# Where split weights and activations start inside a partition of SBUF, in a float32r transformer block

## The chip, the cores and the metric

The kernel runs on one core of a Trainium2 chip. The metric is device time in microseconds (us). The kernel before took 2280.99 us, the median of three runs (2273.52 to 2281.04).

## The reference

One residual block on x (256 tokens x 2048), all in float32, every part wrapped in RMSNorms:

```
h = rmsnorm(x);  x = x + 0.5 * rmsnorm((silu(h @ w_gate) * (h @ w_up)) @ w_down)      # FFN 1, width 5632
h = rmsnorm(x)
proj = h @ w_in                     # forgetting attention q,k,v,f; differential attention q,k,v; memory q
y_fox, y_diff, y_mem = three attentions over 256 tokens (the last over 256 memory tokens)
gates = sigmoid(h @ w_merge_gate + b)                                                  # 3 x 2048
merged = g_fox * (y_fox @ w_fox) + g_diff * (y_diff @ w_diff) + g_mem * (y_mem @ w_mem)
x = x + rmsnorm(merged @ w_out)
h = rmsnorm(x);  x = x + 0.5 * rmsnorm((silu(h @ w_gate2) * (h @ w_up2)) @ w_down2)    # FFN 2
```

The weights are over 400 MB; each is read once. The bulk of the arithmetic is matrix products of 256 tokens with these weights.

## The kernel before, in words

**Split operands.** A float32 operand is used as two float32r parts, hi (the rounded value, written by ScalarE) and lo (the rest, written by VectorE). Weights come by DMA in tiles of 128 partitions x 2048 values (`raw`, three buffers). `Stream.ahead` (lines 71 to 94) splits each half of such a tile into a `hi` and a `lo` tile of 1024 values, in four buffers each, or, for three pieces of the `out` projection, in buffers of an extra pool. Activations are kept transposed as tiles `[P, k, 2, 256]`: for each block k of 128 channels a row of 256 hi values and a row of 256 lo values, 2048 bytes in all.

**Two forms of product.** `mm_a` (lines 193 to 198) has a 128x128 block of a weight stationary and streams activations. First hi of the weight against the 512 columns hi and lo of the activation, then lo of the weight against the 256 hi columns. This pair is called a pair below. `mm_b` (lines 231 to 240) has a 128x128 block of an activation stationary and streams weights: three products of 512 columns (428 in the projection `v`): hi by hi, hi by lo, lo by hi. This is called a triple.

**Stages in order.** FFN 1 gate and up (`mm_a` on `hT1`, 1408 pairs); FFN 1 down (`mm_b` on `gh1`); memory keys and values (`mm_b` on `mha`, `mhb`); projection `v` (`mm_b` on `h2T`, width 428); queries, keys and merge gates (`mm_a` on `h2T`, 1088 pairs) with the branch products (`mm_a` on `y_a`, `y_b`, 128 pairs each) and the attentions between them; `out` (`mm_b` on `mT`); FFN 2 gate and up (`mm_a` on `h3T`, 1408 pairs); FFN 2 down (`mm_b` on `gh2`). By the loops that makes 4160 pairs, 2688 streamed products of 512 columns in `mm_b` and 576 of 428 columns.

**What sets the order.** The schedule is written by hand: each engine runs its instructions in the order of the program text. TensorE takes a weight piece once ScalarE and VectorE have split it; `Stream` loads and splits ahead as far as buffers are free.

**Where tiles lie.** The pools place tiles one behind the other in each partition; nothing asks for more than the pools' default. In the built program of the kernel before, the byte address in the partition at which a tile starts, modulo 256, is:

| tile | role in mm_a | role in mm_b | start mod 256, before |
|---|---|---|---|
| hi, lo (4 buffers each) | stationary | streamed | 224 |
| hi, lo of the extra pool (3 each) | - | streamed in `out` | 192 |
| second 428-wide row of a piece of `v` | - | streamed | 144 |
| hT1 | streamed | - | 192 |
| h2T | streamed | stationary in `v` | 128 |
| h3T | streamed | - | 128 |
| y_a / y_b | streamed | - | 192 / 128 |
| mha / mhb | - | stationary | 192 / 128 |
| gh1 / gh2 | - | stationary | 128 / 192 |
| mT | - | stationary | 128 |

Inside a tile the stationary blocks step by 512 bytes and the streamed activation rows by 2048, so that within a pair the start of the streamed row less that of the weight block, modulo 1024, alternates between two values: 480 and 992 for hT1 and y_a, 160 and 672 for h2T, h3T and y_b.

Of the kernel before, what the change touches and what calls it, by code (L numbers as in the profile page):

```python
# [8 lines left out]
F32 = mybir.dt.float32  # L9
F32R = mybir.dt.float32r  # L10
BF16 = mybir.dt.bfloat16
AF = mybir.ActivationFunctionType
ALU = mybir.AluOpType
# [3 lines left out]
P = 128  # L17
D = 2048
S = 256
KT = D // P  # L20
FF = 5632
FT = FF // P
NB = 428
EPS = 1e-6
LAM_INIT = 0.8 - 0.6 * math.exp(-0.3 * 0)
NEG = -1e30

C_G1, C_GM, C_GMEM, C_G2, C_B, C_HG = 0, 16, 32, 48, 64, 112
N_COLS = 113
# [2 lines left out]
class Stream:  # L32
# [33 lines left out]
    def ahead(self, most=8):  # L66

        for _ in range(most):
            if self.done == len(self.plan):
                break  # L70
            _, r, half, extra = self.plan[self.done]
            if extra:
                if self.extra_pool is None:
                    break
                pool, tag = self.extra_pool, "x"
            else:
                if sum(not p[3] for p in self.plan[self.used:self.done]) == self.split_bufs:
                    break
                pool, tag = self.split_pool, ""
            self.load()  # L80
            w = self.aps[r].shape[-1] // 2
            src = self.raw[r][:, half * w:(half + 1) * w]
            hi = pool.tile([P, D // 2], F32R, tag="hi" + tag, name="hi")
            lo = pool.tile([P, D // 2], F32R, tag="lo" + tag, name="lo")
            n = 2 if self.done == 0 else 1
            for i in range(n):
                o = slice(i * w // n, (i + 1) * w // n)
                self.nc.scalar.copy(out=hi[:, o], in_=src[:, o])  # L88
                self.nc.vector.tensor_tensor(out=lo[:, o], in0=src[:, o], in1=hi[:, o].bitcast(F32), op=ALU.subtract)  # L89
            self.split[self.done] = (hi, lo)  # L90
            self.left[r] -= 1
            if not self.left[r]:
                del self.raw[r]
            self.done += 1
        self.load()
# [16 lines left out]
def tile_block(ctx, tc, x, mem, f1gu, f1d, wqk, wv, wmkv, wgate, wbr, wout, f2gu, f2d,  # L112
               cols, rows, lamv, fbias, cf, cb, rope, out):
    nc = tc.nc
# [74 lines left out]

    fill = Fillers(3, 2)  # L190


    def mm_a(bank, w, kk, act, k, start, stop):

        hi, lo = w
        nc.tensor.matmul(bank, lhsT=hi[:, kk * P:(kk + 1) * P], rhs=act[:, k].rearrange("p s n -> p (s n)"),  # L196
                         start=start, stop=False)
        nc.tensor.matmul(bank[:, 0:S], lhsT=lo[:, kk * P:(kk + 1) * P], rhs=act[:, k, 0], start=False, stop=stop)  # L198

    def new_bank(name):  # L200
        return mmp.tile([P, 512], F32, tag="mm", name=name)
# [27 lines left out]
    def mm_b(bank, piece, w, act, t, k0, start, stop):  # L229

        hi, lo = piece
        for kk in range(2):
            xh = act[:, k0 + kk, 0, t * P:(t + 1) * P]
            xl = act[:, k0 + kk, 1, t * P:(t + 1) * P]
            wh = hi[:, kk * w:(kk + 1) * w]
            wl = lo[:, kk * w:(kk + 1) * w]
            o = bank[:, 0:w]
            nc.tensor.matmul(o, lhsT=xh, rhs=wh, start=start and kk == 0, stop=False)  # L238
            nc.tensor.matmul(o, lhsT=xh, rhs=wl, start=False, stop=False)  # L239
            nc.tensor.matmul(o, lhsT=xl, rhs=wh, start=False, stop=stop and kk == 1)  # L240
# [42 lines left out]
    def rstd_of(acc, n, name):  # L283
# [3 lines left out]
        nc.vector.reduce_sum(out=ms, in_=acc, axis=AX.X)  # L287
        nc.vector.tensor_scalar(out=ms, in0=ms, scalar1=1.0 / n, scalar2=EPS, op0=ALU.mult, op1=ALU.add)
        rsqrt(r, ms)
# [45 lines left out]
    class PostProj:  # L335
# [24 lines left out]
        def body(self):  # L360
# [6 lines left out]
            for t in range(2):  # L367
                ssq = small.tile([P, 1], F32, tag="ssq", name="ssq_post")
                self.base[t] = small.tile([P, 1], F32, tag="base", name="base")
                nc.vector.reduce_sum(out=ssq, in_=self.acc[t][:, 0:3], axis=AX.X)  # L370
                nc.vector.tensor_scalar(out=self.base[t], in0=ssq, scalar1=f / D, scalar2=f * EPS,
                                        op0=ALU.mult, op1=ALU.add)
# [62 lines left out]
    hpool = h1_stack.enter_context(tc.tile_pool(name="hT1", bufs=1, side="right", reuse_waits="tile"))  # L435
    tp1 = h1_stack.enter_context(tc.tile_pool(name="ft1", bufs=1, side="right", reuse_waits="tile"))
    gp1 = g1_stack.enter_context(tc.tile_pool(name="gh1", bufs=1, side="left", reuse_waits="tile"))
    hT1 = hpool.tile([P, KT, 2, S], F32R, name="hT1")
    gh1 = gp1.tile([P, FT, 2, S], F32R, name="gh1")

    def load_x(c):
        for t in range(2):
# [25 lines left out]
    yap = ya_stack.enter_context(tc.tile_pool(name="yap", bufs=1, side="right", reuse_waits="tile"))  # L468
    fg_stack = ExitStack()
    fgp = fg_stack.enter_context(tc.tile_pool(name="fg1", bufs=1, side="right", reuse_waits="tile"))  # L470
    mha = yap.tile([P, 8, 2, S], F32R, tag="y", name="mha")
    macc = [small.tile([P, 4], F32, name=f"macc{t}", bufs=1) for t in range(2)]
    order = [(c, t) for c in range(4) for t in range(2)]
    mem_c = {}
# [27 lines left out]
    h2_stack = ExitStack()  # L502
    h2p = h2_stack.enter_context(tc.tile_pool(name="h2p", bufs=1, side="left", reuse_waits="tile"))
    ybp = yb_stack.enter_context(tc.tile_pool(name="ybp", bufs=1, side="left", reuse_waits="tile"))
    h2T = h2p.tile([P, KT, 2, S], F32R, tag="h", name="h2T")
    mhb = ybp.tile([P, 8, 2, S], F32R, tag="y", name="mhb")

    def x1_update(i):
        if i < 8:
# [158 lines left out]

        return [s1, s2]

    y_a = yap.tile([P, 8, 2, S], F32R, tag="y", name="y_a")
    y_b = ybp.tile([P, 8, 2, S], F32R, tag="y", name="y_b")

    def softmax_stats(s_aps, tag="e", bufs=6):

# [60 lines left out]
    def diff_unit(h):  # L736
# [22 lines left out]
        def s3():  # L759
# [12 lines left out]
            f = (1.0 - LAM_INIT) ** -2  # L772
            nc.vector.tensor_scalar(out=ms, in0=ms, scalar1=f / P, scalar2=f * EPS, op0=ALU.mult, op1=ALU.add)
            rsqrt(r, ms)
# [40 lines left out]
    for n in range(6):  # L815
        banks = proj_b("v", h2T, KT, NB)
        if n == 0:
            hrow = row_of(hr, h2p)
        for a, b, dst in segs:
            lo_c, hi_c = max(a, n * NB), min(b, (n + 1) * NB)  # L820
            if lo_c < hi_c:
                for t in range(2):
                    o, i = dst(t, lo_c - a, hi_c - a), banks[t][:, lo_c - n * NB:hi_c - n * NB]
                    if t == 0:
# [30 lines left out]
    mT = None  # L855
    for m in range(KT):
        zs = []
        for b in range(3):
            z = zp.tile([P, S], F32, tag="z", name="z", bufs=4)
            lr_sum(z, proj_a("gate", h2T), zp)  # L860
            times_row(z, hrow)
            zs.append(z)
        if m == 0:
            while fill.left():
                fill(drain=True)
            at_stack.close()
            mgp = mg_stack.enter_context(tc.tile_pool(name="mgp", bufs=1, side="left", reuse_waits="tile"))
            mT = mgp.tile([P, KT, 2, S], F32R, name="mT")
        bb = [new_bank("mm_br") for _ in range(3)]
        lims = [(0, 8), (8, 12), (12, 16)]  # L870
        for half in range(2):
            st.ahead()
            w, = st.take("br")
            for kk in range(8):
                k = half * 8 + kk
                i = 0 if k < 8 else (1 if k < 12 else 2)
                mm_a(bb[i], w, kk, (y_a, y_b)[half], kk, k == lims[i][0], k == lims[i][1] - 1)
            st.release()
        acc = None
        for b in range(3):  # L880
            g = zs[b]
            c = C_B + b * KT + m
            nc.scalar.activation(out=g, in_=g, func=AF.Sigmoid, bias=colt[:, c:c + 1])
            br = zp.tile([P, S], F32, tag="br", name="br")
            lr_sum(br, bb[b], zp)
            nc.vector.tensor_tensor(out=g, in0=br, in1=g, op=ALU.mult)
            if acc is not None:
                nc.vector.tensor_tensor(out=g, in0=acc, in1=g, op=ALU.add)
            acc = g
        split_to(mT[:, m, 0], mT[:, m, 1], acc)  # L890
# [1 line left out]
    ya_stack.close()  # L892


    h3T = h2p.tile([P, KT, 2, S], F32R, tag="h", name="h3T")
    fg_stack = ExitStack()
    fgp = fg_stack.enter_context(tc.tile_pool(name="fgm", bufs=1, side="right", reuse_waits="tile"))
    st.extra_pool = fg_stack.enter_context(tc.tile_pool(name="xsplit", bufs=3, side="right", reuse_waits="tile"))
# [28 lines left out]
    def setup2():  # L927
        row = row_of(h3r, h2p)
        fg_stack.close()
        mg_stack.close()  # L930
        yb_stack.close()
        tp = tp2_stack.enter_context(tc.tile_pool(name="ft2", bufs=1, side="left", reuse_waits="tile"))
        gp = g2_stack.enter_context(tc.tile_pool(name="gh2", bufs=1, side="right", reuse_waits="tile"))
        return row, tp, gp.tile([P, FT, 2, S], F32R, name="gh2")

    gh2 = ffn_up(2, h3T, lambda: h3r.extend(token_rstd(x_sb, t) for t in range(2)), setup2,
                 {1: lambda: (splits.pop(0)(), post2.update(1, 2), st.ahead(1)), 2: lambda: (turn(2), post2.update(1, 3)),
                  4: lambda: (splits.pop(0)(), st.ahead(1)), 5: lambda: turn(3), 8: lambda: splits.pop(0)(),
                  10: lambda: st.ahead(2)})
# [96 lines left out]
```

## Time and profile before

| | us |
|---|---|
| median of three runs | 2280.99 |
| the profiled execution | 2281.44 |
| its span, first to last instruction | 2279.6 |
| TensorE matmul busy | 2260.3 (99%) |
| TensorE weight load busy | 1939.0 (85%) |
| VectorE busy | 1407.3 (62%) |
| ScalarE busy | 1104.3 (48%) |
| DMA engines, mean share of queue 1 | 52.3% |

A busy share says how much of the span had at least one instruction of the engine under way. A matmul's listed duration includes a tail in which the next one already streams, so that durations add up to more than the time; how far one start lies from the next is the number to read. "L196" is line 196 of the kernel; the same line of the changed kernel has a larger number.

### The profile page before, as it was taken

What the parts mean: (1) busy time and instruction counts of PE and PEld (TensorE: products, weight loads), DVE (VectorE), ACT (ScalarE), POOL (GpSimd) and SP (SyncE); (2) the same over time, 40 slices, a digit from 0 to 9 for tenths busy, and PEclk for the clock granted to TensorE, in tenths of its full rate; (3) what the DMA queues carried; (4) which work ended last, traced back from release to release, by engine and by line L of the source; (5) the groups of instructions that cost most, each with busy time, mean ns of one, the idle gap of its engine ahead of it and who ended that gap; (6) DMA issues with size and microseconds to landing.
All of it is one profiled execution on the core that took longest, in us unless ns stands there. A gap on an engine that the chain in (4) does not pass through costs nothing. (4 is left out here: it accounts for less than half of the span.)

```text
span 2279.6 us, 30353 instructions
## 1 busy us (share of the span) xinstructions
PE 2260.3 (99%) x12028; PEld 1939.0 (85%) x12028; DVE 1407.3 (62%) x1969; ACT 1104.3 (48%) x1704; POOL 11.4 (0%) x22
## 2 busy tenths in 40 slices
PE   8999999999999999999999999999999999999998
PEld 7888888888888899888888888878888888888886
DVE  6666666665444656766776767566666666654444
ACT  6444444444433554444555555446544544443342
POOL 0000000000000000000000000000000000000000
PEclk9999999999999999999999999999999999999999
DMA  6555555556555554444555555545555555555553
GB/s 224 189 187 189 189 188 186 185 185 217 192 193 198 176 175 162 165 159 155 178 185 188 182 203 178 203 155 203 185 187 194 193 185 189 197 193 192 196 196 129
DMA packets 63646, 423.15 MB, mean 186 GB/s; under 512 B 7440, under 2 KB 7824, under 8 KB 16144
## 3 DMA queue, kind: packets, MB, share of 16 engines
q1 hardware_dynamic: 59616, 415.33, 52.3%
q10 hardware_dynamic: 3888, 5.88, 0.8%
q8 instruction: 94, 1.54, 0.3%
q14 instruction: 48, 0.39, 0.1%
HBM read 419.09 MB, written 2.10 MB: 185 GB/s over the span
## 5 line engine op out<-in xcount | busy, mean ns | idle before, releaser
L89 DVE TENSOR_TENSOR lo<-raw,hi 128x1024 fp32r<-128x1024 f32 (+2 forms) x793 | 942.8, 1211 | 469.7 <-ACT hi L88 426.2
L88 ACT CAST hi<-raw 128x1024 fp32r<-128x1024 f32 (+2 forms) x793 | 814.7, 1039 | 397.8 <-PE mm_b L240 322.5
L196 PE MATMUL mm_a<-hT,hi 128*128 128x512 f32 x1408 | 499.7, 398 | 2.9 <-DVE hT L321 2.9
L196 PE MATMUL mm_a<-h3T,hi 128*128 128x512 f32 x1408 | 489.7, 392 | 1.0 <-DVE h3T L321 1.0
L198 PE MATMUL mm_a<-hT,lo 128*128 128x256 f32 x1408 | 397.5, 282 | 0.9 <-DVE lo L89 0.9
L198 PE MATMUL mm_a<-h3T,lo 128*128 128x256 f32 x1408 | 394.0, 280 | 0.0
L196 PE MATMUL mm_a<-h2T,hi 128*128 128x512 f32 x1088 | 384.1, 395 | 0.0
L196 PEld LDWEIGHTS mm_a<-hT,hi 128*128 128x128 f32 x1408 | 265.1, 188 | 68.7 <-ACT hi L88 3.5
L196 PEld LDWEIGHTS mm_a<-h3T,hi 128*128 128x128 f32 x1408 | 264.9, 188 | 59.6 <-ACT tg L313 1.2
L198 PE MATMUL mm_a<-h2T,lo 128*128 128x256 f32 x1088 | 304.2, 280 | 0.0
L238 PE MATMUL mm_b<-hi,gh 128*128 128x512 f32 x704 | 279.7, 397 | 0.0
L394 ACT ACTIVATE left<-mm_a 128x256 f32<-128x256 f32 x244 | 93.8, 384 | 382.3 <-PE mm_a L198 382.3
L240 PE MATMUL mm_b<-hi,gh 128*128 128x512 f32 x704 | 277.7, 394 | 0.0
L239 PE MATMUL mm_b<-lo,gh 128*128 128x512 f32 x704 | 277.2, 394 | 0.0
L198 PEld LDWEIGHTS mm_a<-hT,lo 128*128 128x128 f32 x1408 | 266.1, 189 | 2.2 <-DVE lo L89 2.2
L198 PEld LDWEIGHTS mm_a<-h3T,lo 128*128 128x128 f32 x1408 | 264.8, 188 | 0.1
L196 PEld LDWEIGHTS mm_a<-h2T,hi 128*128 128x128 f32 x1088 | 204.4, 188 | 43.8
L198 PEld LDWEIGHTS mm_a<-h2T,lo 128*128 128x128 f32 x1088 | 204.4, 188 | 0.2
L240 PEld LDWEIGHTS mm_b<-hi,gh 128*128 128x128 f32 x704 | 132.1, 188 | 33.4
L239 PEld LDWEIGHTS mm_b<-lo,gh 128*128 128x128 f32 x704 | 132.1, 188 | 31.5
L238 PEld LDWEIGHTS mm_b<-hi,gh 128*128 128x128 f32 x704 | 132.1, 188 | 31.3
L396 DVE TENSOR_TENSOR up<-mm_a,left 128x256 f32<-128x256 f32 x88 | 37.3, 424 | 75.9 <-ACT left L394 75.9
(205 smaller groups left out, 1781.0 us busy)
## 6 DMA issues: line engine op xcount, KB each, us to landing
raw<-in_f2gu SPq DMA_DIRECT2D x88, 1024.0 KB, 4.8
raw<-in_f1gu SPq DMA_DIRECT2D x86, 1024.0 KB, 4.8
raw<-in_wgate SPq DMA_DIRECT2D x48, 1024.0 KB, 4.7
raw<-in_f1d SPq DMA_DIRECT2D x44, 1024.0 KB, 4.8
raw<-in_f2d SPq DMA_DIRECT2D x44, 1024.0 KB, 4.7
raw<-in_wv SPq DMA_DIRECT2D x24, 856.0 KB, 4.5
raw<-in_wqk SPq DMA_DIRECT2D x20, 1024.0 KB, 4.8
raw<-in_wbr SPq DMA_DIRECT2D x16, 1024.0 KB, 4.7
```

Source lines behind the costliest of these rows:

```text
L88: self.nc.scalar.copy(out=hi[:, o], in_=src[:, o])
L89: self.nc.vector.tensor_tensor(out=lo[:, o], in0=src[:, o], in1=hi[:, o].bitcast(F32), op=ALU.subtract)
L196: nc.tensor.matmul(bank, lhsT=hi[:, kk * P:(kk + 1) * P], rhs=act[:, k].rearrange("p s n -> p (s n)"), start=start, stop=False)
L198: nc.tensor.matmul(bank[:, 0:S], lhsT=lo[:, kk * P:(kk + 1) * P], rhs=act[:, k, 0], start=False, stop=stop)
L238: nc.tensor.matmul(o, lhsT=xh, rhs=wh, start=start and kk == 0, stop=False)
L239: nc.tensor.matmul(o, lhsT=xh, rhs=wl, start=False, stop=False)
L240: nc.tensor.matmul(o, lhsT=xl, rhs=wh, start=False, stop=stop and kk == 1)
L394: nc.scalar.activation(out=left, in_=bank[:, 0:S], func=AF.Copy, scale=scale)
L396: nc.vector.tensor_tensor(out=dst, in0=bank[:, S:2 * S], in1=left, op=ALU.add)
```

## The change

No tile gets other contents and no instruction is added or taken away. In the built programs each engine has the same instructions in the same order with the same waits; the one difference in shape is that the 96 splits of `v` pieces are written as 2 rows of 428 instead of one of 856. What differs is where tiles start.

- Pieces `hi` and `lo` start at a multiple of 256 bytes (`align_bytes=LINE`). A `v` piece starts 32 bytes behind one, and its second row 1792 bytes (448 values) behind the first.
- `rows_of` makes the activation tiles 32 bytes longer and starts them at a multiple of 256 bytes (offset 0) or 32 bytes behind one (`OFF`, 8 values): offset 32 for hT1, h2T, h3T, y_a and y_b, offset 0 for gh1, gh2, mT, mha and mhb.
- The scratch area for dynamic DMA descriptors, at the start of each partition, is 4096 bytes instead of 16384, and the tiles behind it move up.

In the built program of the changed kernel the addresses modulo 256 are 0 for hi and lo, also those of the extra pool, 32 for both rows of a `v` piece, 32 for hT1, h2T, h3T, y_a and y_b, and 0 for gh1, gh2, mT, mha and mhb. Within a pair, the streamed row's start less the weight block's, modulo 1024, alternates between 32 and 544 in all of `mm_a`.

```diff
+NBS = 448
+LINE = 256
+OFF = 8
@@ Stream.ahead
-            w = self.aps[r].shape[-1] // 2
-            src = self.raw[r][:, half * w:(half + 1) * w]
-            hi = pool.tile([P, D // 2], F32R, tag="hi" + tag, name="hi")
-            lo = pool.tile([P, D // 2], F32R, tag="lo" + tag, name="lo")
-            n = 2 if self.done == 0 else 1
-            for i in range(n):
-                o = slice(i * w // n, (i + 1) * w // n)
-                self.nc.scalar.copy(out=hi[:, o], in_=src[:, o])
-                self.nc.vector.tensor_tensor(out=lo[:, o], in0=src[:, o], in1=hi[:, o].bitcast(F32), op=ALU.subtract)
+            w = self.aps[r].shape[-1] // 4
+            off, step = (OFF, NBS) if w == NB else (0, w)
+            src = self.raw[r][:, half * 2 * w:(half + 1) * 2 * w].rearrange("p (k n) -> p k n", k=2)
+            hi, lo = (pool.tile([P, D // 2], F32R, tag=t + tag, name=t, align_bytes=LINE)[:, off:off + 2 * step]
+                      .rearrange("p (k n) -> p k n", k=2)[:, :, 0:w] for t in ("hi", "lo"))
+            for i in range(2) if self.done == 0 else (slice(0, 2),):
+                self.nc.scalar.copy(out=hi[:, i], in_=src[:, i])
+                self.nc.vector.tensor_tensor(out=lo[:, i], in0=src[:, i], in1=hi[:, i].bitcast(F32), op=ALU.subtract)
@@ tile_block
+    def rows_of(pool, n, off, **kw):
+        t = pool.tile([P, n * 2 * S + OFF], F32R, align_bytes=LINE, **kw)
+        return t[:, off:off + n * 2 * S].rearrange("p (k s n) -> p k s n", k=n, s=2)
...
-        nc.tensor.matmul(bank, lhsT=hi[:, kk * P:(kk + 1) * P], rhs=act[:, k].rearrange("p s n -> p (s n)"),
+        i, c = kk // 4, slice(kk % 4 * P, (kk % 4 + 1) * P)
+        nc.tensor.matmul(bank, lhsT=hi[:, i, c], rhs=act[:, k].rearrange("p s n -> p (s n)"),
                          start=start, stop=False)
-        nc.tensor.matmul(bank[:, 0:S], lhsT=lo[:, kk * P:(kk + 1) * P], rhs=act[:, k, 0], start=False, stop=stop)
+        nc.tensor.matmul(bank[:, 0:S], lhsT=lo[:, i, c], rhs=act[:, k, 0], start=False, stop=stop)
...
-            wh = hi[:, kk * w:(kk + 1) * w]
-            wl = lo[:, kk * w:(kk + 1) * w]
+            wh, wl = hi[:, kk], lo[:, kk]
...
-    hT1 = hpool.tile([P, KT, 2, S], F32R, name="hT1")
-    gh1 = gp1.tile([P, FT, 2, S], F32R, name="gh1")
+    hT1 = rows_of(hpool, KT, OFF, name="hT1")
+    gh1 = rows_of(gp1, FT, 0, name="gh1")
...
-    y_a = yap.tile([P, 8, 2, S], F32R, tag="y", name="y_a")
-    y_b = ybp.tile([P, 8, 2, S], F32R, tag="y", name="y_b")
+    y_a = rows_of(yap, 8, OFF, tag="y", name="y_a")
+    y_b = rows_of(ybp, 8, OFF, tag="y", name="y_b")
...
-            mT = mgp.tile([P, KT, 2, S], F32R, name="mT")
+            mT = rows_of(mgp, KT, 0, name="mT")
...
-    nc = bacc.Bacc("TRN2", target_bir_lowering=False, num_devices=1)
+    nc = bacc.Bacc("TRN2", target_bir_lowering=False, num_devices=1, dynamic_dma_scratch_size=4096)
```

The tiles h2T and h3T (`OFF`), mha, mhb and gh2 (offset 0) are changed in the same way as those shown.

## Rows read from the trace of the kernel before

**Rows 1.** The page: busy time of an engine, share, instructions; slices of TensorE's granted clock.
```profile
PE 2260.3 (99%) x12028; PEld 1939.0 (85%) x12028; DVE 1407.3 (62%) x1969; ACT 1104.3 (48%) x1704; POOL 11.4 (0%) x22
...
PEclk9999999999999999999999999999999999999999
```

**Rows 2.** Waits of PE: line, who released it, us in total, times, longest.
```profile
PE tr_h L311 <- DMA ident<-in_cf: 4.5, 1, 4.5
PE mm_a L196 <- DVE hT L321: 2.9, 2, 2.7
PE tr_h L311 <- DVE x_sb L388: 2.6, 1, 2.6
PE mm_a L196 <- DVE h3T L321: 1.0, 1, 1.0
PE mm_a L198 <- DVE lo L89: 0.9, 2, 0.7
```

**Rows 3.** Stages (FFN 1 up, `v`, FFN 2 up): length, busy us (instructions) per engine, clock, DMA.
```profile
9.40:514.70 505.30, 504.09 (x2844) 437.27 (x2845) 328.22 (x457) 257.75 (x393) 1.11 (x2) 1.00 0.55 189
812.90:940.70 127.80, 127.80 (x676) 118.53 (x674) 78.33 (x160) 59.80 (x102) 1.40 (x2) 1.00 0.51 176
1534.40:2025.60 491.20, 491.19 (x2828) 432.13 (x2829) 325.00 (x452) 251.08 (x380) 1.10 (x2) 1.00 0.54 189
```

**Rows 4.** Line 196 alone in three stretches: length, PE busy (matmuls), PEld busy, clock, DMA.
```profile
60.00:510.00 450.00, 450.00 (x1275) 238.97 (x1274) 1.00 0.55 186
1148.00:1436.00 288.00, 288.00 (x830) 155.61 (x830) 1.00 0.54 190
1575.00:2025.00 450.00, 450.00 (x1300) 243.73 (x1299) 1.00 0.55 190
```

**Rows 5.** Instructions of PE in order of time, FFN 1: start, duration, line, operands.
```profile
200.24 0.40 PE L196 MATMUL mm_a<-hT,hi 128*128 128x512 f32 x1
200.48 0.28 PE L198 MATMUL mm_a<-hT,lo 128*128 128x256 f32 x1
200.60 0.39 PE L196 MATMUL mm_a<-hT,hi 128*128 128x512 f32 x1
200.83 0.28 PE L198 MATMUL mm_a<-hT,lo 128*128 128x256 f32 x1
200.95 0.40 PE L196 MATMUL mm_a<-hT,hi 128*128 128x512 f32 x1
```

**Rows 6.** Line 239 alone in FFN 2 down (columns as in Rows 4, without PEld).
```profile
2030.00:2260.00 230.00, 129.88 (x329) 1.00 0.53 186
```

**Rows 7.** `out`, pieces in the extra pool: first and last of ten starts.
```profile
1510.26 0.39 PE L238 MATMUL mm_b<-hi,mT 128*128 128x512 f32 x1
...
1512.32 0.39 PE L238 MATMUL mm_b<-hi,mT 128*128 128x512 f32 x1
```

**Rows 8.** `out`, pieces in the four usual buffers: first and last of ten starts.
```profile
1513.72 0.39 PE L238 MATMUL mm_b<-hi,mT 128*128 128x512 f32 x1
...
1515.82 0.39 PE L238 MATMUL mm_b<-hi,mT 128*128 128x512 f32 x1
```

**Rows 9.** Projection `v`: first and last of six starts.
```profile
859.71 0.36 PE L238 MATMUL mm_b<-hi,h2T 128*128 128x428 f32 x1
...
860.68 0.36 PE L240 MATMUL mm_b<-hi,h2T 128*128 128x428 f32 x1
```

**Rows 10.** Splits in `v`, us 790 to 935: form, count, busy us, mean ns, idle before.
```profile
L89 DVE TENSOR_TENSOR lo<-raw,hi 128x856 fp32r<-128x856 f32 x48 | 50.2, 1048 | 34.6 <-ACT hi L88 34.2
L88 ACT CAST hi<-raw 128x856 fp32r<-128x856 f32 x48 | 43.2, 907 | 30.7 <-PE mm_b L240 30.7
```

**Rows 11.** DMA queues of the page: packets, MB, share.
```profile
q1 hardware_dynamic: 59616, 415.33, 52.3%
q10 hardware_dynamic: 3888, 5.88, 0.8%
q8 instruction: 94, 1.54, 0.3%
q14 instruction: 48, 0.39, 0.1%
```

More of the change, by code (lines that the diff above doesn't have):

```diff
@@ L470, in tile_block @@
     fgp = fg_stack.enter_context(tc.tile_pool(name="fg1", bufs=1, side="right", reuse_waits="tile"))
-    mha = yap.tile([P, 8, 2, S], F32R, tag="y", name="mha")
+    mha = rows_of(yap, 8, 0, tag="y", name="mha")
     macc = [small.tile([P, 4], F32, name=f"macc{t}", bufs=1) for t in range(2)]
@@ L504, in tile_block @@
     ybp = yb_stack.enter_context(tc.tile_pool(name="ybp", bufs=1, side="left", reuse_waits="tile"))
-    h2T = h2p.tile([P, KT, 2, S], F32R, tag="h", name="h2T")
-    mhb = ybp.tile([P, 8, 2, S], F32R, tag="y", name="mhb")
+    h2T = rows_of(h2p, KT, OFF, tag="h", name="h2T")
+    mhb = rows_of(ybp, 8, 0, tag="y", name="mhb")
     def x1_update(i):
@@ L892, in tile_block @@
     ya_stack.close()
-    h3T = h2p.tile([P, KT, 2, S], F32R, tag="h", name="h3T")
+    h3T = rows_of(h2p, KT, OFF, tag="h", name="h3T")
     fg_stack = ExitStack()
@@ L933, in setup2 @@
         gp = g2_stack.enter_context(tc.tile_pool(name="gh2", bufs=1, side="right", reuse_waits="tile"))
-        return row, tp, gp.tile([P, FT, 2, S], F32R, name="gh2")
+        return row, tp, rows_of(gp, FT, 0, name="gh2")
     gh2 = ffn_up(2, h3T, lambda: h3r.extend(token_rstd(x_sb, t) for t in range(2)), setup2,
```

## The prediction

> **What bounds the kernel now.** I read the page's busy times first: TensorE has a matmul under way for 2260.3 of 2279.6 us, at a granted clock of full speed (2.4 GHz) in every slice [rows 1]. Then the waits of PE: together they come to 11.9 us, most of it at the first instruction, at the start of FFN 1 and at the turn to FFN 2 [rows 2]. So TensorE's own pace sets the time, and neither a DMA nor a split that is a little faster or slower would move it. What is left to read is the pace of each stage, as the distance from one matmul's start to the next.
>
> Two stages run the same 1408 pairs on the same weight buffers: FFN 1 up takes 505.3 us and FFN 2 up 491.2 us [rows 3]. Away from their starts, 1275 pairs fill 450 us in the one and 1300 in the other, with no gap: 352.9 against 346.2 ns a pair [rows 4]. The gate stage, most of whose pairs stream h2T, has 830 pairs in 288 us, 347.0 ns [rows 4]. The clock is 1.00 in all three and DMA share 0.54 to 0.55 (same rows). What differs between FFN 1 and FFN 2 is the address of the streamed rows: 192 modulo 256 in hT1, 128 in h3T and h2T. In order of time the slow stage shows two kinds of pair by turns: 200.24 to 200.60 and 200.60 to 200.95, with 0.24 and 0.12 us, then 0.23 and 0.12 between starts [rows 5]. That turn follows the two distances of streamed row from weight block, 480 and 992. If the quicker kind costs what FFN 2's pairs cost, the slower one costs 2 x 352.9 - 346.2 = 359.6 ns. So placement counts, and both halves of the change touch it.
>
> `mm_b` says the same. FFN 2 down has 329 triples in 230 us, so 233.0 ns a product of 512 columns [rows 6]. In `out` nine products from the usual buffers (224 modulo 256) take 1513.72 to 1515.82, 233.3 ns each [rows 8], and nine from the extra pool (192), with the same stationary tile, 1510.26 to 1512.32, 228.9 ns each [rows 7]. Ten starts are a small sample, read to 10 ns, so 4.4 ns is good to about 1.5.
>
> **The change part by part.** The instructions and their order stay; only addresses move.
>
> `mm_b`, 512 columns. Streamed pieces go from 224 to 0 modulo 256, stationary blocks from 128 or 192 to 0. The nearest row is the extra pool's: both operands at multiples of 64. I take its 228.9 against 233.2, the mean of the other two: 4.3 ns for 2652 products (2688 less the 36 that already lie so), 11.4 us. Bounds: no gain, if it was 192 and not the multiple of 64 that counted; or a further step of the same size, 23 us. A loss of 4 ns each (11 us) isn't excluded by a row either.
>
> `mm_a`. The weights go from 224 to 0, the streamed rows from 192 or 128 to 32. No row shows this pair of addresses. The distance between the two, which alternates 480/992 or 160/672, becomes 32/544 everywhere. Bounds from the two ends that the rows show: all pairs at 346.2 ns, or all at 359.6. Three of the four known distances run at the low price, and 32 lies nearest to 992 (64 bytes off, low price). 544 lies 64 bytes off 480, the slow one, and 128 off 672, a quick one. In FFN 2 down, where the distances are 32 and 544 too, products run at 233.0, no worse than elsewhere. I take the low price for all: 1408 pairs of hT1 and 128 of y_a gain 6.7 ns, 10.3 us; the 2624 pairs on h2T, h3T and y_b gain nothing.
>
> `v`. Six starts from 859.71 to 860.68 give 194 ns for 428 columns, with streamed rows at 224 and 144 by turns [rows 9]. They come to lie at 32, the stationary h2T at 32. If its products move by the same 2% as the pairs, it is 576 x 4 ns = 2.3 us either way; I take 0.
>
> The splits of `v` as 2 rows of 428: 48 on VectorE at 1048 ns and 48 on ScalarE at 907 ns [rows 10]. I cost them at nothing: in that stage the engines are busy for 78.3 and 59.8 of 127.8 us, under TensorE's 127.8 [rows 3]. Even 10% on each would be 5 us of idle time used up; it would count only if TensorE began to wait for them. The smaller scratch area costs nothing: the queues are hardware ones and those for instructions [rows 11], and none uses it.
>
> Sum: 10.3 + 11.4 = 21.7 us off the profiled execution's 2281.4 (its span and 1.8 us around it), 2260 us. The profiled execution is 0.5 us above the median of the runs, so it stands for it as it is. With the two main terms each between half and one and a half times, the forecast's own range is 2248 to 2271.
>
> **The rivals.**
>
> *The weight read and the streamed rows hold each other up far less.* At 2.4 GHz a product of 512 columns would stream in 213.3 ns and a pair in 320. The rows have 233.2 and, as the mean over all 4160 pairs, 348.7: 20 and 29 ns more. If good addresses halve that, and the 16 ns over 178.3 in `v`, it is 4160 x 14.3 + 2688 x 10 + 576 x 7.9 = 91 us: 2190. For it: an address already moves these numbers by 4 to 13 ns, and no row has both operands of `mm_a` at the new places. Against: at all placements seen, some 13 ns stay on a product of 512 and 26 on a pair, as if they belonged to the instruction. The Trainium skill ("TensorE: Matmul & The Clock Gate", Back-to-back issue gap) gives N / 2.4 + 2.5 ns from start to start on a warm engine, so 215.8 and 109.2 ns; by that as the floor for every product, an estimate, the time would be about 2128 us. The trace does not agree: at full clock no stage here is under 346.2 ns a pair, where the rule says 325.
>
> *The places don't matter, or the gains cancel.* If half of all pairs fall into the slow kind, as in FFN 1 now, the 2624 quick pairs lose 6.7 ns (17.6 us) against 11.4 from `mm_b`: 2287. If starts modulo 64 and not 256 are all that counts and `mm_b`'s sample misled me, it is 2281 as it was. For it: 544 lies next to the slow 480. Against: both samples of rows 4 and 7 to 8 differ by address alone. The Trainium skill speaks for this case too: "SBUF — State Buffer" (Who interferes with whom) has TensorE read the stationary and the moving operand through two independent ports and says that it waits for nobody; by that, any multiple of 32 bytes is as good and the time stays 2281 us. The trace disagrees, 352.9 against 346.2 ns.
>
> *All pairs fall into the slow kind (slower).* One mechanism: with the row 32 bytes behind the block, the read of the next weights meets the streamed row in each pair, as it does in every second pair of FFN 1. Then 1536 pairs lose 6.7 ns and 2624 lose 13.4: 45.5 us, less 11.4 from `mm_b`, +34: 2315. For it: in `mm_b`, rows that start 32 bytes off a multiple of 64 are the dearer ones (233.3 against 228.9), and `mm_a`'s rows move from a multiple of 64 to just such a place. Against: FFN 2 down has the same distances at the common price. It decides from a mean pair of 354.2 ns on, that is, when 60% of the pairs are slow: then `mm_b`'s gain is gone and 11.4 us lost.
>
> **How the numbers follow.** The measurement tells 0.5%, 11.4 us, from no change. Forecast 0.36; far less hold-up 0.20; no change 0.25; slow pairs 0.19. Faster: 0.20 and nearly all of the 0.36, so 0.54; within 0.5%: 0.25 and the rest, 0.27; slower 0.19. The range for 8 in 10 leaves out a tenth on either side, half of each outer case: from 2195, just above the middle of the first rival, to 2310, just below that of the last. The forecast alone: 2248 to 2271.
>
> **What would show it.** In the changed kernel the FFN 1 and FFN 2 stretches of 450 us should both hold about 1300 pairs of line 206's form, without the turn of 0.36 and 0.35 us. FFN 2 down should have about 335 triples in 230 us where there were 329, and `v` should last 127.8 us within 2.5. TensorE should still be busy for 99%, with the same few waits. The forecast fails if the gate stage or FFN 2 up runs over 347 ns a pair, if FFN 1 up falls clearly under 346, or if `mm_b` stays at 233; each of the three points to one rival.

## The result, and the profile after

The changed kernel takes 2256.3 us (median of four runs, 2256.04 to 2256.76) where the kernel before takes 2281.01 (median of four, 2273.52 to 2282.3): a ratio of 0.9899, 95% interval 0.9877 to 0.992. The profiled execution took 2256.76 us, 24.7 less than before.

The page of the changed kernel, busy times and granted clock (answers to [rows 1]):

```profile
PE 2235.5 (99%) x12028; PEld 1947.3 (86%) x12028; DVE 1408.1 (62%) x1969; ACT 1097.8 (49%) x1704; POOL 11.3 (1%) x22
...
PEclk9999999999999999999999999999999999999999
```

The instructions are as many as before, the clock is full, and TensorE is still the bound. Its waits in the changed kernel, as in [rows 2]:

```profile
PE tr_h L320 <- DMA ident<-in_cf: 4.1, 1, 4.1
PE mm_a L206 <- DVE hT L330: 2.9, 2, 2.7
PE tr_h L320 <- DVE x_sb L397: 2.6, 1, 2.6
PE mm_a L208 <- DVE lo L93: 1.1, 3, 0.7
PE mm_a L206 <- DVE h3T L330: 1.0, 1, 1.0
PE tr_h L320 <- DMA x_sb<-in_x: 0.3, 1, 0.3
```

They sum to 12.0 us against 11.9, so no wait went away: TensorE's pace changed. The stages of the changed kernel in order (FFN 1 up, FFN 1 down, memory, `v`, gates and branches, `out`, FFN 2 up, FFN 2 down), columns as in [rows 3]:

```profile
9.30:506.00 496.70, 495.29 (x2845) 438.20 (x2845) 328.40 (x457) 253.13 (x393) 1.11 (x2) 1.00 0.57 193
506.00:747.20 241.20, 241.20 (x1074) 199.76 (x1073) 117.59 (x111) 103.99 (x128) 0.05 (x1) 1.00 0.60 204
747.20:796.50 49.30, 49.30 (x241) 40.71 (x240) 39.36 (x61) 37.12 (x90) 3.88 (x6) 1.00 0.46 163
796.50:925.00 128.50, 128.50 (x676) 119.20 (x674) 78.68 (x160) 59.89 (x102) 1.40 (x2) 1.00 0.51 175
925.00:1421.80 496.80, 496.80 (x2901) 439.31 (x2900) 344.45 (x547) 249.80 (x426) 1.38 (x2) 1.00 0.51 178
1421.80:1515.70 93.90, 90.33 (x410) 74.28 (x409) 55.39 (x70) 43.82 (x73) 1.11 (x2) 1.00 0.52 185
1515.70:2008.00 492.30, 492.30 (x2828) 436.36 (x2829) 325.33 (x452) 250.14 (x380) 1.09 (x2) 0.99 0.54 188
2008.00:2247.00 239.00, 239.00 (x1057) 197.90 (x1056) 113.09 (x104) 94.22 (x101) 0.55 (x1) 1.00 0.54 187
```

Against the same stages of the kernel before:

| stage | before, us | after, us | gained |
|---|---|---|---|
| FFN 1 up (mm_a on hT1) | 505.3 | 496.7 | 8.6 |
| FFN 1 down (mm_b on gh1) | 248.2 | 241.2 | 7.0 |
| memory keys and values (mm_b) | 50.0 | 49.3 | 0.7 |
| v (mm_b, 428 wide) | 127.8 | 128.5 | -0.7 |
| gates and branches (mm_a) | 497.5 | 496.8 | 0.7 |
| out (mm_b on mT) | 96.2 | 93.9 | 2.3 |
| FFN 2 up (mm_a on h3T) | 491.2 | 492.3 | -1.1 |
| FFN 2 down (mm_b on gh2) | 246.2 | 239.0 | 7.2 |

Line 206 (the 196 of before) alone, in FFN 1, the gates and FFN 2, and line 248 (239 of before) in FFN 2 down, answers to [rows 4] and [rows 6]:

```profile
50.00:500.00 450.00, 450.00 (x1299) 243.71 (x1299) 1.00 0.56 191
1132.00:1420.00 288.00, 288.00 (x831) 155.94 (x832) 1.00 0.54 190
1550.00:2000.00 450.00, 450.00 (x1299) 243.73 (x1299) 1.00 0.55 192
...
2012.00:2242.00 230.00, 131.53 (x339) 1.00 0.54 187
```

FFN 1 has 1299 pairs in 450 us instead of 1275, one less than FFN 2 had before. All three stretches of `mm_a` now run at 346.4 to 346.6 ns a pair; the count is good to one pair, 0.3 ns. FFN 2 down (`mm_b`) has 339 triples in 230 us instead of 329, 226 ns a product; that count is good to one triple, 0.7 ns. In order of time, FFN 1 of the changed kernel, as [rows 5], and nine products of `out`:

```profile
200.24 0.39 PE L206 MATMUL mm_a<-hT,hi 128*128 128x512 f32 x1
200.47 0.28 PE L208 MATMUL mm_a<-hT,lo 128*128 128x256 f32 x1
200.59 0.39 PE L206 MATMUL mm_a<-hT,hi 128*128 128x512 f32 x1
200.81 0.28 PE L208 MATMUL mm_a<-hT,lo 128*128 128x256 f32 x1
200.93 0.39 PE L206 MATMUL mm_a<-hT,hi 128*128 128x512 f32 x1
...
1499.74 0.39 PE L249 MATMUL mm_b<-hi,mT 128*128 128x512 f32 x1
...
1501.78 0.39 PE L249 MATMUL mm_b<-hi,mT 128*128 128x512 f32 x1
```

The turn of 0.36 and 0.35 us is gone: pairs take 0.35 and 0.34, read to 10 ns. The nine products take 2.04 us, 226.7 ns each, against 233.3 in [rows 8] and 228.9 in [rows 7].

### The profile page after: what moved, and what is told of

The parts are those of the page before. It is cut to its first block, busy times and chain, and to the rows that moved or that the text cites. A ratio compares the mean times of both kernels' runs of the same rounds, so it can differ in the third digit from the quotient of the medians.

```text
span 2255.0 us, 30353 instructions
## 1 busy us (share of the span) xinstructions
PE 2235.5 (99%) x12028; PEld 1947.3 (86%) x12028; DVE 1408.1 (62%) x1969; ACT 1097.8 (49%) x1704; POOL 11.3 (1%) x22
## 5 line engine op out<-in xcount | busy, mean ns | idle before, releaser
L206 PE MATMUL mm_a<-hT,hi 128*128 128x512 f32 x1408 | 490.7, 391 | 2.9 <-DVE hT L330 2.9
L247 PE MATMUL mm_b<-hi,gh 128*128 128x512 f32 x704 | 274.2, 390 | 0.0
L249 PE MATMUL mm_b<-hi,gh 128*128 128x512 f32 x704 | 273.9, 389 | 0.0
```

The source lines that it names most:

```text
L206: nc.tensor.matmul(bank, lhsT=hi[:, i, c], rhs=act[:, k].rearrange("p s n -> p (s n)"), start=start, stop=False)
```

## The experiments

One word is used for all of them. The *distance* is the start of the streamed operand less the start of the stationary block that is loaded beside it, modulo 256 bytes. In the kernel before it was 224 in FFN 1 up, 160 in the gates and FFN 2 up, 96 in FFN 1 down and `out`, 32 in FFN 2 down. In the changed kernel it is 32 in all of `mm_a` and 0 in `mm_b`. Modulo 256 the steps inside a tile drop out, so that each stage has one distance (but `v` in the kernel before). The diffs are against the changed kernel and shortened; offsets are given as lists, in values of 4 bytes.

**Weights only** (`e1_weights_only`). The activations go back to their old places modulo 256.

```diff
-hT1 OFF, h2T OFF, h3T OFF, y_a OFF, y_b OFF, gh1 0, gh2 0, mT 0, mha 0, mhb 0
+hT1 48, h2T 32, h3T 32, y_a 48, y_b 32, gh1 32, gh2 48, mT 32, mha 48, mhb 32     # in values of 4 bytes
```

> Half of the change: the split weights start at multiples of 256 (v pieces 32 behind), the activations lie where they lay before modulo 256 (hT1, y_a, mha, gh2 at 192, the others at 128). Three theories. Own start: a streamed operand is dearer when it starts 32 bytes off a multiple of 64, whatever the stationary block does; then mm_b has its whole gain (226.7 ns a product of 512) and mm_a is as in the kernel before (FFN 1 352.9 ns a pair, FFN 2 346.2), about 2263 us. Stationary: the place of the stationary block alone counts; then mm_b stays at 233 and FFN 1 falls to 346.8, about 2272 us. Distance: the streamed start less the stationary one, modulo 1024, decides; mm_b then has 64 to 896 instead of 0 and 512, and lies at neither 226.7 nor 233 by any rule known so far.

Measured: 2287.27 us, ratio to before 1.0053 (1.0034 to 1.0073). Half of the change is slower than none. Line 206 in FFN 1 and FFN 2 up, line 248 in FFN 2 down:

```profile
50.00:500.00 450.00, 450.00 (x1275) 239.47 (x1274) 1.00 0.55 188
...
1560.00:2010.00 450.00, 450.00 (x1283) 240.80 (x1282) 1.00 0.53 189
...
2042.00:2272.00 230.00, 129.96 (x335) 1.00 0.53 186
```

FFN 1 stays at 352.9 ns a pair although its stationary blocks now start at multiples of 256; FFN 2 up loses, 350.7 after 346.2, although its streamed rows lie at 128 modulo 256 as before. So neither operand's own place alone decides `mm_a`. FFN 2 down comes to 228.9, half way.

**Activations only** (`e2_activations_only`). The other half.

```diff
-            off, step = (OFF, NBS) if w == NB else (0, w)
+            off, step = 0, w
-            hi, lo = (pool.tile([P, D // 2], F32R, tag=t + tag, name=t, align_bytes=LINE)...
+            hi, lo = (pool.tile([P, D // 2], F32R, tag=t + tag, name=t)...
```

> The other half: the activations lie as in the changed kernel (32 behind a multiple of 256 where mm_a streams them, at a multiple where mm_b holds them), the weights start at 224 modulo 256 as before. Own start: mm_b stays at 233 ns a product (its streamed weights start at 224), and mm_a gets dearer than 347 ns a pair because its rows now start 32 off a multiple of 64; about 2290 us or more. Stationary: mm_b falls to 226.7, mm_a's blocks are at 224 as before, 346 to 353; about 2265 us. Distance: mm_a has 64/576 in FFN 1 and 320/832 in the gates and FFN 2, none of them seen; 346 to 360.

Measured: 2299.65 us, ratio 1.0106 (1.0082 to 1.013). Line 206 in FFN 2 up and line 248 in FFN 2 down:

```profile
1560.00:2010.00 450.00, 449.68 (x1273) 239.05 (x1273) 1.00 0.53 185
...
2050.00:2280.00 230.00, 129.95 (x329) 1.00 0.53 185
```

FFN 2 up 353.5 ns a pair, FFN 2 down 233.0 a product as before. Stationary blocks at multiples of 256 gain nothing by themselves. The two halves cost 0.5% and 1.1% and together gain 1%: the cost hangs on both places at once.

**Both moved by 96 bytes** (`e5_both_moved_96`). Every place of the changed kernel is given up, the distances are kept.

```diff
+            off, step = (32, NBS) if w == NB else (24, w)      # weights 96 bytes behind a multiple of 256, v pieces 128
+            hi, lo = (pool.tile([P, D // 2 + 24], F32R, tag=t + tag, name=t, align_bytes=LINE)...
+hT1, h2T, h3T, y_a, y_b: 32 values = 128 bytes;  gh1, gh2, mT, mha, mhb: 24 values = 96 bytes
```

> All split weights and stationary activations start 96 bytes behind a multiple of 256 and all streamed activations and v pieces 128 behind one, so the distance from stationary to streamed start, modulo 256, is what the changed kernel has (32 in mm_a, 0 in mm_b), at other places. Distance theory: the pace is that of the changed kernel, 346.8 ns a pair and 226.7 ns a product of 512. Places theory (a multiple of 256 of the stationary block's start is what counts): both fall back to 233 and 350 to 353.

Measured: 2255.73 us in one run, beside 2281.78 for before. Line 206 in FFN 1 and FFN 2, line 248 in FFN 2 down:

```profile
50.00:500.00 450.00, 450.00 (x1299) 243.56 (x1299) 1.00 0.56 192
...
1550.00:2000.00 450.00, 450.00 (x1299) 243.73 (x1299) 1.00 0.55 192
...
2012.00:2242.00 230.00, 131.64 (x339) 1.00 0.53 186
```

Each count is that of the changed kernel. With no operand at a multiple of 256, the whole gain is there: what it needs is the distance, and "a multiple of 256 bytes" was only a way to fix it. That these distances count modulo 256, and not modulo 512 or 1024, shows here too: the weight tiles are 96 bytes longer (4192, rounded up to 4352), so that in the built program the pieces in the four buffers start at 96, 352, 608 and 864 modulo 1024, and the counts stay.

**Other distances** (`e6_distances_a`, `e7_distances_b`, `e8_distances_c`). Only the offsets of the activations differ, weights at multiples of 256.

```diff
+e6: hT1 40, h2T 24, h3T 16, y_a 56, y_b 48, gh1 16, gh2 24, mT 40, mha 8, mhb 56
+e7: hT1 4, h2T 12, h3T 20, y_a 28, y_b 36, gh1 4, gh2 12, mT 20, mha 28, mhb 36
+e8: hT1 44, h2T 52, h3T 60, y_a 24, y_b 16, gh1 44, gh2 52, mT 60, mha 40, mhb 48
```

> The changed kernel with other offsets of the activations; weights at multiples of 256. In mm_a the streamed row lies behind the stationary block, modulo 256, by 160 (FFN 1), 96 (gates), 64 (FFN 2), 224 (y_a), 192 (y_b); in mm_b by 192 (FFN 1 down), 160 (FFN 2 down), 96 (out). Distance theory, from the earlier kernels with the same distance at other places: 160 gives 346.2 to 346.5 ns a pair (FFN 2 before), 64 gives 353 (activations only), 224 and 192 give 353 (before; weights only); mm_b at 96 gives 233 (before). Places theory: the streamed start alone has to explain it, and 64, 160 and 224, which are or are not multiples of 64, sort otherwise: 64 the quickest, 160 and 224 the slowest.

> As the last, with distances not seen so far: in mm_a 16 (FFN 1), 48 (gates), 80 (FFN 2), 112 (y_a), 144 (y_b); in mm_b 240, 208 and 176. No theory has a number. If the pace follows the distance smoothly, 16 and 48 lie beside the 346.8 of 32. If nothing under 346 ns a pair turns up in this and the next kernel, the change's 32 is among the best there are.

> As the last: in mm_a 176 (FFN 1), 208 (gates), 240 (FFN 2), 96 (y_a), 64 (y_b); in mm_b 80 (FFN 1 down), 48 (FFN 2 down), 16 (out). y_a and y_b repeat the distances of gates and FFN 2 of e6 in another stage and must agree with them if the distance decides; 240 and 16 in mm_b lie beside the 226.7 of 0.

Measured, one run each: 2288.97, 2296.22 and 2285.28 us. Line 206 of e6 in FFN 1 up (distance 160) and FFN 2 up (64):

```profile
50.00:500.00 450.00, 450.00 (x1299) 243.56 (x1299) 1.00 0.56 191
...
1550.00:2000.00 450.00, 449.68 (x1273) 239.08 (x1273) 1.00 0.53 186
```

Both are what kernels with other places and these distances had: 160 the 346 of FFN 2 before, 64 the 1273 pairs of "activations only". Line 206 of e7 in FFN 1 up (distance 16) is the worst:

```profile
50.00:500.00 450.00, 450.00 (x1251) 238.75 (x1251) 1.00 0.54 184
```

The same expectation missed once: the distance 224 of `y_a` in e6 was to give 353, as in FFN 1 before. Its 128 pairs come in 16 groups of 8, of which the first pair is longer; the first and the last start of the other seven, in the first group and in the second:

```profile
1093.05 0.39 PE L206 MATMUL mm_br<-y_a,hi 128*128 128x512 f32 x1
...
1095.17 0.39 PE L206 MATMUL mm_br<-y_a,hi 128*128 128x512 f32 x1
...
1115.49 0.39 PE L206 MATMUL mm_br<-y_a,hi 128*128 128x512 f32 x1
...
1117.57 0.39 PE L206 MATMUL mm_br<-y_a,hi 128*128 128x512 f32 x1
```

Six pairs take 2.12 us in the first group, 353 ns each, and 2.08 us in the second, 347 ns, and so in all later groups: one distance, the same rows of `y_a`, and two paces in one execution. So the distance narrows the pace down and does not fix it.

The FFN stretches of 450 us by distance, as 450 us over the count of line 206; each entry is one execution, good to one pair, 0.3 ns:

| distance in mm_a | ns a pair, kernel and stage |
|---|---|
| 0 | 346.4 (e3, FFN 1), 352.9 (e3, FFN 2); see the next run |
| 16 | 359.7 (e7, FFN 1) |
| 32 | 346.4 (changed, FFN 1 and 2; e5, both) |
| 64 | 353.5 (e2, FFN 2; e6, FFN 2), 352.9 (e2, FFN 1) |
| 80 | 353.2 (e7, FFN 2) |
| 128 | 350.7 (e1, FFN 2) |
| 160 | 346.2 (before, FFN 2), 346.4 (e6, FFN 1) |
| 176 | 349.7 (e8, FFN 1) |
| 192 | 352.9 (e1, FFN 1) |
| 224 | 352.9 (before, FFN 1) |
| 240 | 353.2 (e8, FFN 2) |

Nothing is under the 346 that 32 and 160 have in every stretch, and 16 bytes away from 32 lies the dearest. In FFN 2 down, 230 us hold 339 triples at distance 0 (changed, e5), 335 at 64 (e1), 332 at 48 (e8), 329 at 32, 208 and 224 (before, e7, e2) and 328 at 160 (e6). So the best distance isn't the same for the two forms of product: 160 is among the best for `mm_a` and the dearest here for `mm_b`.

**No offset** (`e3_no_offset`). Distance 0 everywhere.

```diff
-hT1, h2T, h3T, y_a, y_b: OFF
+hT1, h2T, h3T, y_a, y_b: 0
-            off, step = (OFF, NBS) if w == NB else (0, w)
+            off, step = (0, NBS) if w == NB else (0, w)
```

> The changed kernel with all offsets 0: every streamed and stationary tile starts at a multiple of 256, also the v pieces. Own start: mm_a is at least as good as with 32, 346.8 ns a pair or less, v too. Stationary: nothing changes, 346.8 and 226.7. Distance: 0 and 512 in mm_a; as mm_b runs at 226.7 with just these, mm_a should gain some 6 ns a product of 512, to about 340; a theory in which stream and weight load meet when both start at the same place says 353 to 360 instead.

Measured: 2270.22 us, ratio 0.9963 (0.9939 to 0.9987), but ten runs lie between 2257.96 and 2275.37, in groups near 2258, 2266 and 2275, where the changed kernel's lie within 0.7 us. Line 206 in FFN 1 and FFN 2 up:

```profile
50.00:500.00 450.00, 450.00 (x1299) 243.38 (x1298) 1.00 0.56 191
...
1550.00:2000.00 450.00, 450.00 (x1275) 239.37 (x1274) 1.00 0.54 187
```

The same distances, weight buffers and form of loop, in one execution at full clock, and 346.4 ns in one stage, 352.9 in the other. So here too a distance has more than one steady pace in `mm_a`, and none of the theories said so. Against this kernel's median the changed kernel, with the 32 bytes of `OFF`, is 14 us quicker and without the spread. But it was not run beside e3, where the kernel before spread as well: six of its 14 runs took 2272.28 to 2273.02 us, the others 2280.58 to 2282.24.

**Short weight loads** (`e4_short_loads`). In FFN 2 the second product of a pair, and the second and third of a triple, use 32 of 128 stationary columns, except the last of a group.

```diff
+        if act is short_of[0] and not stop:
+            nc.tensor.matmul(bank[0:32, 0:S], lhsT=lo[:, i, c][:, 0:32], rhs=act[:, k, 0], start=False, stop=stop)
+            return
...
+            m = 32 if act is short_of[1] and not (stop and kk == 1) else P
+            nc.tensor.matmul(o[0:m], lhsT=xh[:, 0:m], rhs=wl, start=False, stop=False)
+            nc.tensor.matmul(o[0:m], lhsT=xl[:, 0:m], rhs=wh, start=False, stop=stop and kk == 1)
```

> Leaves out part of the computation in FFN 2: the products with the low part of a weight (mm_a) and the second and third product of a triple (mm_b) use 32 of the 128 stationary columns, except the last of a group, so that their weight loads read 128 bytes a partition instead of 512; columns streamed are the same. Line numbers move by a few. If what a product of 512 columns takes above 213.3 ns (15 ns in mm_a, 13 in mm_b) comes from the weight load that is read beside it, the product beside a short load falls to 216 to 218 ns and the others stay; if it belongs to the streamed rows, all stay at 228.4 and 226.7.

Measured: 2258.18 us. The weight loads of FFN 2 up, the full one of `hi` and the short one of `lo`, which runs beside the product of 512 columns (count, busy us, mean ns), and the pace there and in FFN 2 down:

```profile
L207 PEld LDWEIGHTS mm_a<-h3T,hi 128*128 128x128 f32 x1358 | 254.6, 187 | 157.1
L210 PEld LDWEIGHTS mm_a<-h3T,lo 128*32 128x32 f32 x1274 | 137.6, 108 | 0.1
...
1550.00:2000.00 450.00, 450.00 (x1303) 243.96 (x1302) 1.00 0.54 192
...
2012.00:2242.00 230.00, 131.14 (x334) 1.00 0.53 186
```

The load falls from 187 to 108 ns, the pair by 1 ns (345.4), and in FFN 2 down the product gets dearer, 229.5 after 226. So what a product takes above the prediction's 213.3 ns does not follow the length of the load beside it. Whether it belongs to the streamed rows or to each instruction these runs don't tell.

**A distance for each stream** (`e9_own_distances`), and the one that looked best for all of `mm_a` (`e11_low_part_32`).

```diff
+            hi, lo = (pool.tile([P, D // 2 + ...])[:, off + x:off + x + 2 * step]... for t, x in (("hi", 0), ("lo", LO_OFF.get(what, 0))))
+LO_OFF (e9, values): FFN 1 8, qk and gates 40, br 32, FFN 2 56; hT1 8, h2T 40, h3T 0, y_a 8, y_b 8; v pieces 36
+low part's offset (e11): 8 for every piece that mm_a holds; activations as in the changed kernel
```

> The two streams of a pair get distances of their own (the stream's start less the start of the block that is loaded beside it, modulo 256): the 512 columns / the 256 columns are at 0 / 32 in FFN 1, 0 / 160 in the gates, 32 / 0 in FFN 2 and 160 / 32 in the branch products; mm_b stays at 0 and v is at 240. If each stream's cost follows its own distance alone, as mm_b's 226.7 ns at 0 has it, FFN 1 and the gates come to 226.7 + 118.3 = 345 ns a pair, 1.7 ns less, 4 us in all, and FFN 2 stays near 346.7 or above; if the two streams of a pair hang together (the pair takes one of a few lengths, 340, 346.7, 350, 353.3), FFN 1 and gates come out at one of these and can be slower than 346.7.

> The changed kernel with one more offset: the low parts of the weights that mm_a holds start 32 bytes behind a multiple of 256. Beside the 512 columns the low block is loaded, at a distance of 0 then, beside the 256 columns the high block, at 32 as before; as in FFN 1 of the run on own distances (344.7 ns a pair). If that pair of distances is what made the difference there, all of mm_a runs at 344.7 instead of 346.7, 4160 x 2.0 = 8 us under the changed kernel, about 2248 us. If FFN 1's gain was of that stage alone, FFN 2 and the gates stay at 346.7: about 2253 us.

e9 measured 2264.8 us, ratio 0.9925 (0.9908 to 0.9942). Its FFN 1 up (0 beside the 512 columns, 32 beside the 256) was the quickest so far, 344.3 ns a pair, the gates 346.6, FFN 2 up (32 and 0) 353.2. e11, with the best of these everywhere, measured 2259.57 us, ratio 0.9921 (0.9899 to 0.9942), its runs between 2256.55 and 2272.65. Line 208 of e11 in FFN 1, gates and FFN 2:

```profile
50.00:500.00 450.00, 450.00 (x1299) 242.73 (x1298) 1.00 0.56 191
1150.00:1420.00 270.00, 270.00 (x765) 143.44 (x765) 1.00 0.53 186
1550.00:2000.00 450.00, 449.98 (x1308) 244.91 (x1307) 1.00 0.56 192
```

Three paces, 346.4, 352.9 and 344.0, at the same two distances. The 344 exists, but nothing here chooses it; the expectation of 2248 us failed.

**The v pieces at distance 240** (`e10_v_240`).

```diff
-            off, step = (OFF, NBS) if w == NB else (0, w)
+            off, step = (4, NBS) if w == NB else (0, w)
```

> The changed kernel with the v pieces 16 bytes behind a multiple of 256 instead of 32, so that v's distance is 240 instead of 0. By the distance theory v falls from 195.5 to 193.5 ns a product (as with distances b), 128.5 to 127.3 us as a stage, and the rest stays: about 2255 us, 0.05% under the changed kernel. If v's pace hangs on something else it stays at 128.5 us.

Measured: 2256.22 us, ratio 0.9887 (0.9872 to 0.9902). `v` in this kernel, and in e7, which had 240 too:

```profile
796.80:925.30 128.50, 128.50 (x676) 118.54 (x675) 78.64 (x160) 59.89 (x102) 1.40 (x2) 1.00 0.52 175
```

```profile
814.90:942.30 127.40, 127.40 (x677) 118.60 (x675) 78.72 (x160) 59.86 (x102) 1.40 (x2) 1.00 0.53 176
```

A miss: the same distance gave 128.5 and 127.4 us, so the distance alone doesn't decide `v`. Whether it has several paces at one distance, as `mm_a` has, or something else counts with rows of 428 columns stays open; it is about 1 us.

**The changed kernel again** (`e12_changed_again`), on the chip of e11:

> The changed kernel once more, on the same chip as the last, so that the two can be told apart: 2256 us, as before.

2256.61 us (2256.13 to 2256.85), ratio 0.9889 (0.9876 to 0.9902). No kernel tried beats it clearly; it is level with e5 and e10.

## Why the prediction was right

Forecast 2260, measured 2256.3: the cause and the sign held, and the term of `mm_b` was too small.

1. *TensorE's pace is the bound, only addresses move.* Right: waits 12.0 us against 11.9, clock and counts unchanged.
2. *FFN 1 takes the pace of FFN 2, 9.4 us of the 10.3.* Right in size, 8.6: 1299 pairs for 1275. The price came from FFN 2, which ran at 160, and 32 turned out to have the same pace, the lowest that any uniform distance had. That was luck in part: modulo 256 the prediction's four known distances are two, 224 and 160, one at each price, so no row spoke for the low price at 32.
3. *h2T, h3T and y_b gain nothing.* Right but for 1.1 us lost in FFN 2 up.
4. *`mm_b` gains 4.3 ns a product, 11.4 us.* Mis-sized: the four `mm_b` stages of 512 columns gained 7.0 + 0.7 + 2.3 + 7.2 = 17.2 us, 6.5 ns for each of the 2652 products. The row that stood for it [rows 7] was a true sample of another case: its distance is 64, and e1 gives 228.9 at 64 in FFN 2 down; the changed kernel has 0. The bound named for it, a further step of the same size, held it.
5. *`v` 0, within 2.3 us.* It lost 0.7.
6. *The splits of `v` and the scratch area at nothing.* VectorE and ScalarE are busy in `v` for 78.68 and 59.89 us against 78.33 and 59.80.

The saving of FFN 1 is not there against every execution of the kernel before, which the prediction, worked out from one trace, did not see. The distance 224 has the quick pace too (`y_a` in e6), and of the 37 timed runs of the kernel before seven took 2272.28 to 2273.52 us, the others 2280.58 or more. The gap is about FFN 1's 8.6 us; that these seven had the quick pace in FFN 1 is an estimate, since none of them has a trace. Against them the change gains 16 to 17 us, about what all stages but FFN 1 gained here (16.1).

The reason given for the `mm_b` row, both operands at multiples of 64, was wrong; e5, with weights at 96, shows it. So was the reading of [rows 5] as two kinds of pair by distance: 480 and 992 are the same modulo 256, and `y_a` of e6 changes its pace between groups that step through the same rows. The slow rival's argument from a row's own start fell with that, and no run shows the meeting of weight read and streamed row that it named. Its price was no fancy, though: at distance 16 the whole of FFN 1 runs at 359.7, and the rival had it at 359.6. In FFN 1 the change was 16 bytes from being that rival. The no-change rival rested on independent ports, which the Trainium skill states ("SBUF — State Buffer", Who interferes with whom): e1, e2 and e5 show that the pace follows the places of both operands together, so here they do not behave as independent. The first rival's floor never came: no stage of any kernel ran under 344 ns a pair, where "TensorE: Matmul & The Clock Gate" in the Trainium skill (Back-to-back issue gap) has 325, an estimate from its formula, which that section gives for the isolated gap of a single matmul.

Still open: why the distance counts, what chooses among several paces at one distance, and the 13 ns above the prediction's 213.3 that a product of 512 columns keeps.

## What to carry to other kernels

Where TensorE is busy throughout, divide a stage's length by its count of matmuls and compare stages that run the same code; 2% between two such stages with the same clock and no waits means that the operands' places are worth a look. What to set is the distance between streamed and stationary start, not either alignment by itself: either half of this change alone made the kernel slower. Scan several distances in one kernel, one for each stage, but take a single trace for what it is, one of perhaps several paces: repeat the runs, and prefer a distance whose runs agree, as 32 did (eight runs of the changed kernel within 0.9 us), to one that is sometimes quicker. Look at the spread of the kernel before too, since part of a gain can be a pace that it already has in some runs.

## What the runs showed of the hardware

- With other distances modulo 256 between the two operands' starts, float32r products take 346 to 360 ns for a pair of 512 and 256 columns, and 226 to 234 ns for a product of 512, at full clock.
- Shifting both operands by the same 96 bytes left the counts as they were (1299, 1299 and 339).
- At distance 0 one program took near 2258, 2266 or 2275 us in different runs; in the one that was traced, a whole stage ran at 346.4 ns a pair and another at 352.9.
- At distance 224 pairs on the same rows of `y_a` ran at 353 ns in their first group and at 347 from the second on, in one execution (e6).
- A weight load of 32 columns instead of 128 took 108 ns instead of 187 and changed the pair beside it by 1 ns.
